# The two scans run alone with two copies of their staging tiles, and the local attention runs after them with the memory's keys and values between its blocks

## The chip, the cores and the metric

The kernel runs on one core of one Trainium2 chip. The core has a matrix engine (TensorE, PE in the profile), a vector engine (VectorE, DVE), a scalar engine (ScalarE, ACT), GpSimd (POOL) and SyncE (SP). SP issues all the transfers spoken of here, and 16 DMA engines carry them. The metric is the device time of one execution in microseconds.

## The reference, cut to what matters

One layer of an encoder over 2048 tokens of width 1024. One input projection feeds three groups of heads that don't depend on each other. Their results are joined by one output projection; a cross attention to 256 memory tokens and a feed-forward layer follow.

```python
h = rmsnorm(x, norm_mix_w[l])
(na_q, ..., ml_q, ..., gd_q, ...) = jnp.split(h @ w_in[l], IN_OFFSETS, axis=-1)
y_na = neighbourhood_attention(na_q, na_k, na_v, na_rel_bias[l])   # 6 heads of 64, window of 8 x 16 on a 32 x 64 grid
y_ml = mlstm_mixer(ml_q, ml_k, ml_v, ...)                          # 4 heads, one scan in each direction
y_gd = gated_deltanet_mixer(gd_q, gd_k, gd_v, ...)                 # 6 heads, one scan in each direction
x = x + jnp.concatenate([y_na, y_ml, y_gd], axis=-1) @ w_out[l]
x = x + memory_cross_attention(rmsnorm(x, norm_xa_w[l]), rmsnorm(mem, norm_mem_w[l]), w_xq[l], w_xkv[l], w_xo[l])
h = rmsnorm(x, norm_ffn_w[l])
x = x + jnp.square(jax.nn.relu(h @ w_ff1[l])) @ w_ff2[l]
```

## The kernel before

There are three passes. `pass_a` (to about 980 us) makes the input projection and what the scans need, and writes it to HBM: `kb_d`, `g_st`, `gd_c`, `w_d`, `sc_d`, `v_d` for the gated DeltaNet, `mlc_d`, `mlv_d`, `mx_row`, `ai_row` for the mLSTM, `nac_d`, `nav_d` for the local attention, `gate_d` for the output gates.

`pass_b` (about 985 to 1930 us) interleaves four generators:

- `gdn_scan`: 16 steps. Step m treats tile m (128 tokens) in the forward direction and tile 15-m in the backward one, each on its own half of the partitions. `load(m+1)` is written ahead of the step's arithmetic. It loads `wp`, `sc` and `qe` with one or two DMAs for each direction, and `kb` and `ge` with one DMA for both (line 666, in `both`). The source of `ge` is two rows of 768 numbers, one a direction, each read for 64 partitions; the source of `kb` is two blocks of 64 x 768. ScalarE takes the exponential of `ge` (line 647), GpSimd multiplies it into `sc` (line 650), TensorE makes products of `kb` and `wp` (line 658). The step has two halves, one for each chunk of 64 tokens, in a chain of three products and their copies (lines 681 to 702); each half waits for the state of the half before.
- `ml_scan`: the same shape for the mLSTM, with `mkq`, `mr_`, `mqe` and, as one DMA for both directions from two rows of 512 numbers, `mge` (line 851) and `me` (line 850). VectorE and GpSimd work on `me` (lines 852, 853). It runs one step behind (`LAG`).
- `na`: the local attention, 16 blocks of 128 queries. A block holds 6 heads, treated in three pairs; of a head the scores (line 977), bias and minimum (982), exponential (983), transposes (987), copies (990, 992) and the product with the values (997); at its end the sums' reciprocals (1000, 1004) and a store to `y_d` (1009). Bias tiles (947), values (953) and queries (956) are loaded a block ahead; the keys lie in a tile of 24 of the grid's 32 rows that is loaded anew at block 8.
- `heads_out`: for each of 16 tiles, once both directions have reached it, the norm of the heads, the gate `gz` (loaded in line 716) and a store to `y_d`. The first of the tiles can start at step 9.

A scheduler builds one instruction list for each engine from this program; tiles come from pools with a number of buffers (`bufs`), and a load into a tile waits until the last reader of the buffer is done. SP takes its list in order, so a DMA that waits for its buffer holds all the later ones.

After that `tail`: the memory is normed (`mem_in`), its keys and values are computed with `w_xkv` in 16 steps (`mem_kv`: 24 matmuls of 128 x 256 each, line 95), and the cross attention goes through four blocks of 512 tokens (`y_in` reads `y_d`, `mixed` applies `w_out`, then norm, queries, attention, output). In the first block four of the 16 key and value steps stand ahead of `w_out`, ten between the norm and the queries, and two behind them. From there to the end the kernel is matmuls with few gaps.

## Time and profile before

| what | value |
|---|---|
| median of 3 runs | 4131.57 us (4126.9 to 4132.66) |
| the profiled execution | 4129.29 us |
| its span | 4127.3 us |
| mean granted TensorE clock | 0.897 |
| TensorE busy | 3515.8 us (85%) |
| VectorE, ScalarE, GpSimd busy | 43%, 27%, 35% |
| DMA read and written | 331.16 MB, 92.12 MB |

The page cuts the span into 40 slices of 103 us and gives the busy share of each engine in tenths; the row of the granted clock and that of the DMA read alike. The scans are slices 10 to 19:

```
PE   5988999895357566663999999999999999999998
PEclk8989999995576766775999999999999999999999
DMA  4476425855343454533333333321111132111112
```

The chain that ended last is followed back from the last instruction: at each step to what released it. A share of that chain under a DMA's name is time in which the end of the kernel waited for this transfer.

### The profile page before, as it was taken

The numbers are of one execution on the slowest core, as the hardware profiler recorded it, in microseconds if no ns is written. First come the engines' busy times: TensorE is split into PE (matmuls) and PEld (weight loads), VectorE is DVE, ScalarE is ACT, GpSimd is POOL, SyncE is SP. The second block draws the span as 40 slices with busy tenths as digits, with TensorE's granted clock in tenths as the row PEclk, the third lists the DMA queues.
The fourth block names the chain that finished last, engine by engine and source line by source line (L and its number), as shares of the span: only waits on it lengthen the run. The fifth ranks groups of instructions, "written<-read, shape, count | busy, mean of one in ns | idle before, by whom it ended". The sixth has DMA issues, their size and how long they took to land.

```text
span 4127.3 us, 53735 instructions
## 1 busy us (share of the span) xinstructions
PE 3515.8 (85%) x21360; PEld 2830.8 (69%) x21360; DVE 1770.1 (43%) x3241; ACT 1122.2 (27%) x1976; POOL 1435.5 (35%) x876
## 2 busy tenths in 40 slices
PE   5988999895357566663999999999999999999998
PEld 4766777673235454442888888778888877888887
DVE  7767483741243345555443434532222244222224
ACT  3222422231122222221343333322221232221123
POOL 4242523441121112223544544433333354333333
PEclk8989999995576766775999999999999999999999
DMA  4476425855343454533333333321111132111112
GB/s 134 114 197 135 152 83 160 228 117 140 94 113 91 114 144 118 137 110 129 112 97 127 98 120 131 106 78 46 45 49 51 55 104 83 44 46 47 51 51 87
DMA packets 376610, 426.79 MB, mean 103 GB/s; under 512 B 150872, under 2 KB 277544, under 8 KB 374696
## 3 DMA queue, kind: packets, MB, share of 16 engines
q1 hardware_dynamic: 375816, 421.79, 34.8%
q8 instruction: 168, 2.75, 0.3%
q0 software_dynamic: 544, 1.57, 0.2%
q14 instruction: 82, 0.67, 0.1%
HBM read 331.16 MB, written 92.12 MB: 103 GB/s over the span
## 4 chain that ended last, share of the span: by engine, by line
PE 56%; DMA 13%; DVE 4%; SPq 3%; issue 2%; POOL 2%; ACT 1%; DVEq 0%; POOLq 0%; ACTq 0%
PE psg L95 31%; PE psa L95 19%; DMA ge<-g_st 4%; DMA me<-mx_row 3%; DMA wp<-w_d 1%; DMA y_d<-gz 1%; PE psn L977 1%; SPq L953 1%; PE psy L997 1%; PE psn L987 1%; DMA sc<-sc_d 1%; SPq L846 1%; DMA nav<-nav_d 0%; PE pss L688 0%; POOL wlo L1021 0%
## 5 line engine op out<-in xcount | busy, mean ns | idle before, releaser
L1021 POOL TENSOR_TENSOR wlo<-wraw,whi 128x1024 fp32r<-128x1024 f32 (+2 forms) x386 | 773.1, 2004 | 1367.0 <-ACT whi L1019 1328.7
L95 PE MATMUL psg<-acta,whi 128*128 128x512 f32 (+1 forms) x3008 | 951.9, 397 | 6.4 <-ACT acta L1160 3.2
L95 PE MATMUL psg<-actb,whi 128*128 128x512 f32 (+1 forms) x2752 | 841.6, 388 | 49.0 <-ACT actb L273 14.0
L1019 ACT CAST whi<-wraw 128x1024 fp32r<-128x1024 f32 (+2 forms) x402 | 358.1, 891 | 1230.6 <-PE psa L95 556.8
L95 PEld LDWEIGHTS psg<-acta,whi 128*128 128x128 f32 (+1 forms) x3008 | 567.8, 190 | 129.6 <-ACT acta L1160 4.0
L95 PE MATMUL psa<-ht,whi 128*128 128x512 f32 x2048 | 638.7, 395 | 0.7 <-ACT whi L1019 0.7
L95 PEld LDWEIGHTS psg<-actb,whi 128*128 128x128 f32 x2752 | 515.1, 192 | 158.1 <-ACT actb L273 14.7
L95 PE MATMUL psg<-acta,wlo 128*128 128x512 f32 (+1 forms) x1504 | 595.8, 397 | 1.8 <-POOL wlo L1021 1.8
L95 PE MATMUL psg<-actb,wlo 128*128 128x512 f32 (+1 forms) x1376 | 533.0, 387 | 4.7 <-POOL wlo L1021 4.2
L95 PEld LDWEIGHTS psa<-ht,whi 128*128 128x128 f32 x2048 | 384.1, 188 | 95.1 <-ACT whi L1019 1.6
L95 PE MATMUL psa<-ht,wlo 128*128 128x512 f32 x1024 | 400.8, 396 | 0.5 <-POOL wlo L1021 0.5
L1252 DVE TENSOR_TENSOR fr<-fr 128x512 f32<-128x512 f32 x128 | 167.8, 1311 | 495.6 <-ACT fr L1251 495.6
L1265 DVE TENSOR_TENSOR xb<-psa,xb 128x512 f32<-128x512 f32 x256 | 175.6, 691 | 475.9 <-PE psa L95 475.9
L95 PEld LDWEIGHTS psg<-acta,wlo 128*128 128x128 f32 (+1 forms) x1504 | 286.1, 190 | 64.4 <-POOL wlo L1021 3.3
L95 PEld LDWEIGHTS psg<-actb,wlo 128*128 128x128 f32 x1376 | 263.2, 191 | 57.4 <-POOL wlo L1021 5.8
L1255 POOL TENSOR_TENSOR ht<-fr,ht 128x512 fp32r<-128x512 f32 x128 | 168.9, 1320 | 250.2 <-ACT ht L1254 248.9
L95 PEld LDWEIGHTS psa<-ht,wlo 128*128 128x128 f32 x1024 | 192.2, 188 | 47.4 <-POOL wlo L1021 1.7
L853 POOL TENSOR_TENSOR me<-me,gm 128x512 f32<-128x512 f32 x16 | 21.1, 1320 | 456.9 <-DVE me L852 414.4
L987 PE MATMUL psn<-ident,nas 128*96 128x128 f32 (+1 forms) x336 | 75.6, 360 | 111.6 <-ACT nas L983 111.4
L308 DVE SCALAR_TENSOR_TENSOR acc<-pad,vecs,acc 128x512 f32<-128x512 f32 (+2 forms) x144 | 143.8, 1012 | 2.8
L1048 DVE TENSOR_TENSOR ss<-ss,sqt 128x512 f32<-128x512 f32 (+1 forms) x91 | 120.4, 1324 | 45.1 <-ACT sqt L1047 42.2
L997 PE MATMUL psy<-nap,nav 96*64 96x128 f32 (+2 forms) x672 | 89.3, 349 | 52.1 <-ACT nap L990 47.8
(376 smaller groups left out, 4042.3 us busy)
## 6 DMA issues: line engine op xcount, KB each, us to landing
wraw<-in_w_ff SPq DMA_DIRECT2D x72, 512.0 KB
wraw<-in_w_ff SPq DMA_DIRECT2D x144, 256.0 KB
wraw<-in_w_out SPq DMA_DIRECT2D x32, 512.0 KB
wraw<-in_w_xq SPq DMA_DIRECT2D x32, 512.0 KB
wraw<-in_w_xo SPq DMA_DIRECT2D x32, 512.0 KB
wraw<-in_w_gd SPq DMA_DIRECT2D x24, 512.0 KB
sc_d<-sc SPq DMA_DIRECT2D x32, 384.0 KB
sc<-sc_d SPq DMA_DIRECT2D x32, 384.0 KB
```

The costliest lines, as they stand in the source:

```text
L95: nc.tensor.matmul(out=out, lhsT=a(k), rhs=b(k), start=(i == 0), stop=(i == n - 1))
L308: V.scalar_tensor_tensor(out=acc[:, :n], in0=pad[:, p0 + j:p0 + j + n], scalar=cw(j), in1=acc[:, :n], op0=ALU.mult, op1=ALU.add)
L846: nc.sync.dma_start(out=kq[:, d], in_=self.mlc_d[t])
L953: nc.sync.dma_start(out=vw[:rows * ncl, j], in_=src)
L987: nc.tensor.transpose(out=tp[:n, P * j:P * j + P], in_=s[:, kt * j:kt * j + n], identity=self.ident)
L997: nc.tensor.matmul(out=yp[64 * e:64 * e + 64, P * hp:P * hp + P], lhsT=vw[:n, j, 128 * hp + 64 * e:128 * hp + 64 * e + 64], rhs=pts[e][:n, ...
L1019: nc.scalar.copy(out=hi, in_=raw)
L1021: (lo_eng or nc.gpsimd).tensor_tensor(out=lo, in0=raw, in1=hi.bitcast(F32), op=ALU.subtract)
L1048: nc.vector.tensor_tensor(out=ss, in0=ss, in1=sq, op=ALU.add)
L1252: V.tensor_tensor(out=r, in0=r, in1=r, op=ALU.mult)
L1255: G.tensor_tensor(out=ht[:, 1], in0=r, in1=ht[:, 0].bitcast(F32), op=ALU.subtract)
L1265: V.tensor_tensor(out=xs[nb][:, j], in0=ps, in1=xs[nb][:, j], op=ALU.add)
```

## The change

- `pass_b` holds the two scans and `heads_out` only. The pools of PSUM that the local attention had there are gone, `pss` has 4 buffers for 3 and `psl` 3 for 2.
- The staging tiles `kb`, `ge`, `qe`, `mqe`, `mge`, `mkq`, `me` and `gz` have two buffers for one.
- `na` runs in a new `pass_c` at the start of `tail`. It loads all keys with three DMAs (`nak`, 2048 columns a head pair), has four bias tiles for three, its transposes use a PSUM pool of their own (`pst`, 2 buffers) beside that of the scores (`psn`, 2), and the two heads of a pair are written one after the other.
- `mem_in` and `mem_kv` become `self.fill`, of which `pass_c` takes one step with every block of the local attention. The normed memory has its own tile.
- The tiles for the activations and for `x` are allocated after `pass_c`. The first block of the cross attention has nothing to fill the gap at its norm.

Seven lines fewer stand ahead of the scans, so line 647 becomes 640, 666 becomes 659 and so on; line 977 becomes 960 and line 95 becomes 94.

```diff
@@ -220,26 +219,20 @@
 
         with ExitStack() as st:
             pool = lambda name, bufs, **k: st.enter_context(self.pool(name, bufs, **k))
-            self.sps = pool("pss", 3, space=PSUM)
-            self.lps = pool("psl", 2, space=PSUM)
-            self.yps = pool("psy", 1, space=PSUM)
-            self.nps = pool("psn", 2, space=PSUM)
-            attn = self.na(pool("na", 2, side="right"))
+            self.sps = pool("pss", 4, space=PSUM)
+            self.lps = pool("psl", 3, space=PSUM)
             self.acc = pool("acc", 1).tile([P, 16, 10, 64], F32, name="acc")
             scan = self.gdn_scan(pool("scan", 2))
-            next(scan)
+            ml = self.ml_scan(pool("mls", 2))
             out = self.heads_out(pool("out", 2, side="right"))
-            next(out)
-            ml = self.ml_scan(pool("mls", 2))
+            for g in (scan, ml, out):
+                next(g)
             for m in range(16 + LAG):
                 next(scan, None)
                 if m >= LAG:
                     next(ml)
-                self.step(attn, 3)
                 if m - LAG >= 8:
                     self.step(out, 2)
-            for _ in chain(attn, out):
-                pass
 
     def norm_in(self, b):
 
...
@@ -632,9 +625,9 @@
-            kb = pool.tile([P, 2, 6, 64], F32, name="kb", bufs=1)
-            ge = pool.tile([P, 2, 6, 64], F32, name="ge", bufs=1)
-            qe = pool.tile([P, 6, P], F32, name="qe", bufs=1)
+            kb = pool.tile([P, 2, 6, 64], F32, name="kb")
+            ge = pool.tile([P, 2, 6, 64], F32, name="ge")
+            qe = pool.tile([P, 6, P], F32, name="qe")
...
@@ -711,7 +704,7 @@
-            gate = pool.tile([P, 5, P], F32, name="gz", bufs=1)
+            gate = pool.tile([P, 5, P], F32, name="gz")
...
@@ -837,10 +830,10 @@
-            qe = pool.tile([P, 4, P], F32, name="mqe", bufs=1)
-            ge = pool.tile([P, 4, P], F32, name="mge", bufs=1)
-            kq = pool.tile([P, 2, 4, P], F32, name="mkq", bufs=1)
-            e = pool.tile([P, 2, 4, 64], F32, name="me", bufs=1)
+            qe = pool.tile([P, 4, P], F32, name="mqe")
+            ge = pool.tile([P, 4, P], F32, name="mge")
+            kq = pool.tile([P, 2, 4, P], F32, name="mkq")
+            e = pool.tile([P, 2, 4, 64], F32, name="me")
...
@@ -876,6 +869,7 @@
         cur = load(0)
+        yield
...
@@ -921,18 +915,9 @@
-        def keys(parts):
-
-            ks = pool.tile([P, 3, 24 * 64], F32, name="nak", bufs=1)
-            at = 0
-            row = {}
-            for a, b in parts:
-                row.update({r: at + r - a for r in range(a, b)})
-                nc.sync.dma_start(out=ks[:, :, 64 * at:64 * (at + b - a)], in_=self.nac_d[3:6, :, 64 * a:64 * b].rearrange("j p l -> p j l"))
-                at += b - a
-            return ks, row
-
-        ks, row = keys(((4, 28),))
+        ks = pool.tile([P, 3, T], F32, name="nak", bufs=1)
+        for j in range(3):
+            nc.sync.dma_start(out=ks[:, j], in_=self.nac_d[3 + j])
...
@@ -943,7 +928,7 @@
-                    bt = pool.tile([P, 2, 480], F32, name="nab", bufs=3)
+                    bt = pool.tile([P, 2, 480], F32, name="nab", bufs=4)
...
@@ -963,25 +948,22 @@
-            if i == 8:
-                ks, row = keys(((0, 12), (20, 32)))
-            k0 = row[r0]
-                pts, sps = [], [self.nps.tile([P, 512], F32, name="psn") for _ in range(2)]
-                for sp, hb in zip(sps, (slice(0, 64), slice(64, 128))):
-                    nc.tensor.matmul(out=sp[:, :nk], lhsT=q[hb, hp], rhs=grid(ks)[hb, hp, k0:k0 + nr, c0:c0 + ncl], start=True, stop=True)
-                for sp, h in zip(sps, (2 * hp, 2 * hp + 1)):
+                pts = []
+                for h in (2 * hp, 2 * hp + 1):
+                    hb = slice(64 * (h % 2), 64 * (h % 2) + 64)
+                    sp = self.nps.tile([P, 512], F32, name="psn")
+                    nc.tensor.matmul(out=sp[:, :nk], lhsT=q[hb, hp], rhs=grid(ks)[hb, hp, r0:r0 + nr, c0:c0 + ncl], start=True, stop=True)
-                    tp = self.nps.tile([P, 512], F32, name="psn")
+                    tp = self.ntp.tile([P, 512], F32, name="pst")
...
@@ -1065,10 +1047,31 @@
             self.gemm_pools(ctx)
             self.sp = pool("nrm", 2)
             self.yp = pool("yr", 3)
+            self.kv = ExitStack()
+            kv = self.kv.enter_context(self.pool("kv", 1, side="right"))
+            self.kT = kv.tile([P, 2, KT, 256], F32R, name="kT")
+            self.vt = kv.tile([P, 2, 2, 1024], F32R, name="vt")
+            with self.pool("mem", 1) as p:
+                self.fill = chain(self.mem_in(p), self.mem_kv(p))
+                self.pass_c()
+                for _ in self.fill:
+                    pass
+            self.ap = pool("act", 1)
             self.xps = [pool("xa", 1), pool("xb", 1)]
             self.aps = pool("psa", 5, space=PSUM)
             self.cross()
             self.ffn(out)
+    def pass_c(self):
+        with ExitStack() as st:
+            pool = lambda name, bufs, **k: st.enter_context(self.pool(name, bufs, **k))
+            self.yps = pool("psy", 1, space=PSUM)
+            self.nps = pool("psn", 2, space=PSUM)
+            self.ntp = pool("pst", 2, space=PSUM)
+            for i, _ in enumerate(self.na(pool("na", 2, side="right"))):
+                if i % 3 == 1:
+                    self.step(self.fill, 1)
     def xtile(self, i):
         return self.xps[i].tile([P, KT, 512], F32, name="xb")
...
@@ -1089,32 +1092,23 @@
     def cross(self):
         with ExitStack() as ctx:
             self.x2_d = self.dr.tile([4, P, KT, 512], F32, name="x2_d")
-            kv = ctx.enter_context(self.pool("kv", 1))
             self.kp = ctx.enter_context(self.pool("xap", 2))
-            self.kT = kv.tile([P, 2, KT, 256], F32R, name="kT")
-            self.vt = kv.tile([P, 2, 2, 1024], F32R, name="vt")
-            with self.pool("mem", 1) as p:
-                self.mem_in(p)
             prev = None
             for i, b in enumerate(ORDER):
-                with self.pool("mkv", 3) as p:
-                    if i == 0:
-                        fill = self.mem_kv(p)
-                        self.step(fill, KV_FIRST)
-                    xb, ss = self.mixed(b, i)
-                    ha = self.act(0)
-                    self.norm_apply(xb, self.rms_bcast(ss, self.sp), 8, ha, self.sp)
-                    if i > 0:
-                        fill = self.xo(*prev)
-                    self.step(fill, 14 - KV_FIRST if i == 0 else 7)
-                    q = self.queries(ha, 0)
-                    for _ in fill:
-                        pass
+                xb, ss = self.mixed(b, i)
+                ha = self.act(0)
+                self.norm_apply(xb, self.rms_bcast(ss, self.sp), 8, ha, self.sp)
+                fill = self.xo(*prev) if prev else iter(())
+                self.step(fill, 7)
+                q = self.queries(ha, 0)
+                for _ in fill:
+                    pass
                 oa = self.act(1)
                 self.attend(ha, oa, q)
                 prev = b, oa, xb
             for _ in self.xo(*prev):
                 pass
+        self.kv.close()
 
     def mem_in(self, pool):
 
...
@@ -1123,7 +1117,8 @@
-        self.mem = self.act(1)
+        self.mem = pool.tile([P, 2, KT, 256], F32R, name="mem")
+        yield
...
@@ -1138,7 +1133,7 @@
-                tp = self.aps_tile()
+                tp = self.mps.tile([P, 512], F32, name="psm")
```

**SP in the scans.** The five tiles of one load of the DeltaNet scan have neighbouring numbers (`wp_10073`, `sc_10074`, `kb_10075`, `ge_10076`, `qe_10077`). SP before, from `kb` to the local attention's values and its store:

```order
L666 DMA kb_10075<-kb_d_80 128x1x768
L666 DMA ge_10076<-g_st_81 128x1x768
L849 DMA mqe_10215<-mlc_d_74 64x2x128 x4
L851 DMA mge_10216<-ai_row_5956 128x1x512
L956 DMA naqb_9948<-nac_d_76 128x3x128
L641 DMA wp_10073<-w_d01_85 64x768
L641 DMA wp_10073<-w_d12_90 64x768
L846 DMA mkq_10217<-mlc_d_74 128x512 x2
L850 DMA me_10218<-mx_row_5955 128x1x512
L953 DMA nav_9943<-nav_d_77 128x1x384
L1009 DMA y_d1_69<-nat_9685 128x3x128
L953 DMA nav_9943<-nav_d_77 128x1x384 x2
```

SP after, at the same place of a step:

```order
L659 DMA kb_9650<-kb_d_80 128x1x768
L659 DMA ge_9651<-g_st_81 128x1x768
L840 DMA mr__9789<-mlv_d_75 64x2x260 x2
L842 DMA mqe_10300<-mlc_d_74 64x2x128 x4
L844 DMA mge_10301<-ai_row_5956 128x1x512
L634 DMA wp_9393<-w_d01_85 64x768
L634 DMA wp_9393<-w_d12_90 64x768
L839 DMA mkq_10302<-mlc_d_74 128x512 x2
L843 DMA me_10303<-mx_row_5955 128x1x512
```

The local attention's `naqb`, `nav` and `y_d1` are gone from between the scans' loads. Before, `kb` and `ge` of a load stand ahead of the `wp` of that load; after, `kb_9650` and `ge_9651` stand ahead of `wp_9393`, the tile of the load before.

**VectorE at the first norm of the cross attention.** Line 1082 (1085 after) adds a product of `w_out` to `xb`, line 78 (77) begins the norm's factor, line 1037 (1019) applies it; `kT` and `wlo` belong to the memory's keys. VectorE before:

```order
L1082 TENSOR_TENSOR xb<-psg,xb 128x512
L1021 TENSOR_TENSOR wlo<-wraw,whi 128x1024
L1048 TENSOR_TENSOR ss<-ss,sqt 128x512
L1137 TENSOR_TENSOR kT<-psg,kT 128x256
L78 TENSOR_SCALAR ms<-psm 128x4
L1021 TENSOR_TENSOR wlo<-wraw,whi 128x1024
L1137 TENSOR_TENSOR kT<-psg,kT 128x256
L1037 SCALAR_TENSOR_TENSOR nh<-xb,vecs,psm 128x512 x3
L1137 TENSOR_TENSOR kT<-psg,kT 128x256
L1039 TENSOR_TENSOR acta<-nh,acta 128x512
L1037 SCALAR_TENSOR_TENSOR nh<-xb,vecs,psm 128x512 x2
```

VectorE after:

```order
L1085 TENSOR_TENSOR xb<-psg,xb 128x512
L1030 TENSOR_TENSOR ss<-ss,sqt 128x512
L1085 TENSOR_TENSOR xb<-psg,xb 128x512
L1030 TENSOR_TENSOR ss<-ss,sqt 128x512
L77 TENSOR_SCALAR ms<-psm 128x4
L1019 SCALAR_TENSOR_TENSOR nh<-xb,vecs,psm 128x512 x3
L1021 TENSOR_TENSOR acta<-nh,acta 128x512
L1019 SCALAR_TENSOR_TENSOR nh<-xb,vecs,psm 128x512 x3
L1021 TENSOR_TENSOR acta<-nh,acta 128x512
```

Before, work for the keys (`kT`, `wlo`) stands among the norm's instructions; after, only the norm's own do, and the queries (`xq`) come next.

**PE in the local attention.** `psn` are scores, `pst` transposes, `psy` the product with the values, `mem` is the normed memory. PE before, in the scans:

```order
L977 MATMUL psn<-nak,naqb 128x480 x2
L658 MATMUL pss<-wp,kb 64x64 x21
L898 MATMUL psl<-mr__9444,msc 64x65 x8
L658 MATMUL pss<-wp,kb 64x64 x3
L987 MATMUL psn<-ident,nas 128x128 x3
L987 MATMUL psn<-ident,nas 96x128
L681 MATMUL pss<-sc,wp 64x64 x12
L987 MATMUL psn<-ident,nas 128x128 x3
L987 MATMUL psn<-ident,nas 96x128
```

PE after, in its second block:

```order
L960 MATMUL psn<-nak,naqb 128x360
L94 MATMUL psg<-mem,whi 128x256 x3
L94 MATMUL psg<-mem,wlo 128x256
L94 MATMUL psg<-mem,whi 128x256 x2
L94 MATMUL psg<-mem,wlo 128x256
L94 MATMUL psg<-mem,whi 128x256
L979 MATMUL psy<-nap,nav 64x128 x6
L969 MATMUL pst<-ident,nas 96x128 x3
```

The rows of the scans (lines 658 and 681) that filled the places between scores and transposes are gone; rows of `mem` stand there instead, in the first eleven of the 16 blocks.

## Rows read from the trace of the kernel before

**Rows 1.** The page, part 4: the chain that ended last, shares by engine, then by line.
```profile
PE 56%; DMA 13%; DVE 4%; SPq 3%; issue 2%; POOL 2%; ACT 1%; DVEq 0%; POOLq 0%; ACTq 0%
PE psg L95 31%; PE psa L95 19%; DMA ge<-g_st 4%; DMA me<-mx_row 3%; DMA wp<-w_d 1%; DMA y_d<-gz 1%; PE psn L977 1%; SPq L953 1%; PE psy L997 1%; PE psn L987 1%; DMA sc<-sc_d 1%; SPq L846 1%; DMA nav<-nav_d 0%; PE pss L688 0%; POOL wlo L1021
```

**Rows 2.** Waits, 1000 to 1920 us: engine, its line, what released it: total us, times, longest.
```profile
ACT ge L647 <- DMA ge<-g_st: 272.4, 16, 28.3
DVE me L852 <- DMA me<-mx_row: 185.1, 15, 38.8
```

**Rows 3.** Chain of waits, 1280 to 1400 us: start us, length us, what.
```profile
1297.56 19.75 DMA ge<-g_st
...
1325.51 8.94 DMA me<-mx_row
...
1355.37 19.48 DMA ge<-g_st
```

**Rows 4.** Stretches: us, busy us of each engine (instructions), PEclk, DMA share, GB/s.
```profile
1050.00:1790.00 740.00, 452.52 (x5477) 334.93 (x5473) 316.76 (x755) 185.68 (x471) 147.99 (x96) 0.69 0.43 116
1311.00:1316.00 5.00, 0.00 (x0) 0.00 (x0) 0.00 (x0) 0.00 (x0) 0.00 (x0) 0.50 0.13 52
1786.00:1930.00 144.00, 59.80 (x604) 44.15 (x602) 84.42 (x243) 23.52 (x51) 33.97 (x22) 0.62 0.28 86
1968.00:2012.00 44.00, 43.79 (x197) 36.03 (x195) 19.94 (x14) 12.48 (x16) 20.55 (x9) 1.00 0.30 98
```

**Rows 5.** DMA issues, 1050 to 1790 us: out<-in, count, KB each.
```profile
kb<-kb_d SPq DMA_DIRECT2D x14, 384.0 KB
ge<-g_st SPq DMA_DIRECT2D x14, 384.0 KB
...
mge<-ai_row SPq DMA_DIRECT2D x13, 256.0 KB
...
me<-mx_row SPq DMA_DIRECT2D x12, 256.0 KB
...
nav<-nav_d SPq DMA_DIRECT2D x21, 192.0 KB
...
nav<-nav_d SPq DMA_DIRECT2D x22, 144.0 KB
...
naqb<-nac_d SPq DMA_DIRECT2D x13, 192.0 KB
y_d<-nat SPq DMA_DIRECT2D x13, 192.0 KB
```

**Rows 6.** Line 683, 985 to 1930 us: ns min/median/max, first and last start.
```profile
L683 DVE COPY sc<-pss x32: 518/549/551, 1052.2 to 1785.9; 64x384 f32<-64x384 f32 x32
```

**Rows 7.** TensorE by line, 985 to 1930 us, the local attention: count | busy, mean.
```profile
L977 PE MATMUL psn<-nak,naqb 64*128 64x480 f32 (+5 forms) x184 | 95.3, 642 | 0.4 <-ACT nay L1006 0.4
L997 PE MATMUL psy<-nap,nav 96*64 96x128 f32 (+2 forms) x656 | 86.6, 347 | 52.1 <-ACT nap L990 47.8 <-DVE nap L990 4.1
L987 PE MATMUL psn<-ident,nas 128*128 128x128 f32 (+1 forms) x324 | 72.6, 357 | 110.2 <-ACT nas L983 110.0
...
L1004 PE MATMUL psn<-ident,nsm 128*64 128x128 f32 x192 | 19.5, 332 | 10.2 <-DVE nsm L1000 10.2
```

**Rows 8.** Chain of waits, 1786 to 1930 us, the scans' tail.
```profile
1810.71 8.73 DMA me<-mx_row
...
1926.10 2.78 DMA y_d<-gz
```

**Rows 9.** TensorE in order of time, 1940 to 2066 us, memory keys: start us, us, count.
```profile
1963.24 0.40 PE L95 MATMUL psg<-actb,whi 128*128 128x256 f32 x2
...
1966.11 0.40 PE L95 MATMUL psg<-actb,whi 128*128 128x256 f32 x2
```

**Rows 10.** VectorE and ScalarE in order of time, 2008 to 2050 us, the first cross norm.
```profile
2014.93 0.68 DVE L1048 TENSOR_TENSOR ss<-ss,sqt 128x512 f32<-128x512 f32 x1
...
2024.05 1.94 ACT L1038 CAST acta<-nh 128x512 fp32r<-128x512 f32 x3 [0.43 <-DVE nh L1037]
```

More of the change, by code (lines that the diff above doesn't have):

```diff
@@ L35 @@
 ORDER = (1, 2, 0, 3)
-KV_FIRST = 4
 class Trunk:
@@ L138, in gemm_pools @@
         self.wp, self.wb = ctx.enter_context(self.pool("wst", 2, side="right")), 2
-        self.ap = ctx.enter_context(self.pool("act", 1, side="right"))
     def pass_a(self):
@@ L145, in pass_a @@
             self.gemm_pools(st)
+            self.ap = pool("act", 1, side="right")
             self.acts = [None, None]
@@ L1000, in na @@
             V.reciprocal(out=sm, in_=sm)
-            tp = self.nps.tile([P, 512], F32, name="psn")
+            tp = self.ntp.tile([P, 512], F32, name="pst")
             for hp in range(3):
```

## The prediction, made before the changed kernel ran

> **What bounds the kernel now.** I read the chain of waits first. Over half of it is TensorE and 13% are transfers, and the two largest of these belong to the scans, `ge` with 4% and `me` with 3% of the span [rows 1]: some 290 us in which the end of the kernel waited for two small tiles. The change works on the stretch that holds them, the scans, so I ask what sets the pace there. In 740 us of it TensorE is busy for 452 and VectorE for 317, at a granted clock of 0.69; the DMA engines for 0.43 [rows 4]. No engine is the bound by these shares. The waits name the transfers again: ScalarE's line 647 waits 272 us for `ge` in 16 steps and VectorE's line 852 waits 185 us for `me` [rows 2]; one `ge` takes 19 to 20 us at the end of the chain and one `me` 9 [rows 3].
>
> The question that decides the case is why 384 KB take 19 us. From 1311 to 1316 us every engine is idle, ScalarE waits for `ge` (its wait runs from 1297.56 to 1317.31, [rows 3]), and the DMA share is 0.13 with 52 GB/s [rows 4]. 0.13 of 16 engines is two engines. So `ge` is not late because it is issued late; it is slow because two engines carry it. `kb` is written in the same way (two blocks, one for each direction), and so are `me` and `mge`.
>
> A step of the scans takes 47.3 us: the evacuation of line 683 runs from 1052.2 (first half of step 0) to 1785.9 (second half of step 15), which is 15.5 steps [rows 6]. I set this against the two engines. Their own four transfers are 384 + 384 + 256 + 256 KB = 1.31 MB a step [rows 5], at 52 GB/s **25.2 us**. All transfers together keep 0.43 of the engines busy, which is 20.3 us of all 16 for each step; the four take 25.2 x 2/16 = 3.2 of that, and the other 17.1 us, spread over all 16, pass through these two engines too. Sum 42.3 of 47.3 us. The scans before are bound by two DMA engines, with 5 us of slack.
>
> **The change part by part.**
>
> *Doubled tiles.* A second buffer lets `kb`, `ge`, `me` and their like be issued a step earlier, so it hides a delay. It does not make the two engines carry less. It is worth the 5 us of slack at most, and part of it will stay, since `ge` of the next load still stands in one queue behind other tiles that wait for their buffers (in the SP rows `kb_9650` and `ge_9651` come one load ahead of `wp_9393`, and the `sc` of the load before comes after). I take 4 us gained, bounds 0 and 5. `gz` doubled takes its wait out of the tail, below.
>
> The Trainium skill, page "DMA: Bandwidth & Descriptors", section "Why a DMA increments its semaphore by 16 and not by 1", says that a transfer is spread over the largest number of engines up to 16 that divides the slowest dimension of both its sides, and that a transfer issued by an engine's own queue takes the lowest-numbered ones. A source whose outermost dimension is two then runs on two engines, and four such transfers on the same two; the idle stretch with its share of 0.13 agrees with the first half, and no row here shows which engines they are. If the four spread over different pairs, the sum would be that of the first rival.
>
> *The local attention leaves the scans.* Its values, queries and stores are 21 x 192 + 22 x 144 + 13 x 192 + 13 x 192 KB = 12.5 MB in these 740 us [rows 5], 0.8 MB a step of some 4.2 MB that are not the four; bias tiles and keys come on top. I take 5 us of the 17.1, bounds 3 and 7. Its arithmetic beside the scans was not on the path: no engine is full. So a step goes from 47.3 to 47.3 - 4 - 5 = **38 us**, bounds 35 (25.2 + 17.1 - 7, no slack) and 44. From step 9 the heads' `gz` loads and stores join, in fact now in each step: 5 us more, 43. The first two steps find their tiles loaded, and the last two have no loads behind them; for them I go by TensorE's own work, (452 - 275 x 0.8) / 15.7 = 15 us (13 of the 16 blocks lie there) [rows 4, 7], and by 43 on the other side, and take 29. From the first evacuation at 1052: 2 x 29 + 7 x 38 + 4 x 43 + 2 x 29 = 554, so step 15 begins at 1606 and its last half at 1616, against 1785.9. **Gain 170 us**, bounds 60 and 215.
>
> *The tail of the scans.* Before, 142 us pass from 1785.9 to 1928; VectorE is busy for 84 of 144 there, and the rest is waits such as 8.7 us for `me` and 2.8 for a store of `gz` [rows 4, 8]. After, four pairs of heads and three mLSTM steps are left. VectorE's part without the local attention's (some 10 us) for 8 tiles of heads where there were 10 is about 62, and 10 us of waits stay: 72, bounds 60 and 90. The scans end at **1688**, bounds 1630 and 1810, against 1928: 240 us earlier.
>
> *The local attention alone.* This is what it costs. TensorE spent 95 + 87 + 73 + 20 = 275 us on it, at a clock of 0.69 [rows 4, 7], hidden under the scans. At full clock that is 189 us if all of it went with the clock and 275 if none did; I take 205, since matmuls mostly go with it. The memory's keys and values as filler are 8 triples in 2.87 us [rows 9], 128 triples in all, 46 us. So TensorE alone needs 250 us, and it has nothing else to hide behind. The stage cannot be as tight as `w_out` (43.8 busy of 44, [rows 4]): a head is a chain over TensorE, VectorE and ScalarE, line 987 sat idle 110 us for the exponential and line 997 52 us before [rows 7], and the PE rows show that the filler ends with the eleventh of the 16 blocks. I take 300 us, bounds 265 and 360 (some clock lost), and 9 us for its first loads, since keys, bias and values are issued behind the last stores. It ends at 1688 + 9 + 300 = **1997**.
>
> *The join.* Before, the keys and values and 48 matmuls of the queries are done at 2064.9. After, from the end of the local attention: 2.5 us for its last store (a like one took 2.8, [rows 8]), 13 for reading `y_d` behind the loads of `x` (an estimate; in the rows before, the memory's keys hide it), 44 for `w_out` [rows 4], 9 to 12 for the norm, which runs from the last sum at 2014.9 to the first cast at 2024.1 [rows 10] and which nothing covers now, and 16 for the queries. Together 87.5, so the break-even is an end of the local attention at 1977. At 1997 the change **costs 20 us**. From there on the two kernels do the same.
>
> 4129.3 + 20 = 4149 for the profiled execution; the median of the runs before is 2.3 us above it, which makes 4152.
>
> **The rivals.** (a) *Faster.* The scans give more than I take: the two engines are served without a break (35 us a step) and the tail takes 60, so the scans end near 1650, and the local attention stays at full clock with 270 us. It then ends at 1650 + 9 + 270 = 1929, 48 us before the break-even: 4083. If the four slow transfers were on two different pairs of engines, a step's floor would be 25.2 / 2 + 12.1 = 25 us, 13 less in each of 11 steps, and the time about 4010. For it: TensorE is idle for 288 of 740 us in the scans [rows 4], so its own work would allow it. Against it: 42 of 47 us are accounted for by one pair of engines.
>
> (b) *No change.* The same gain in the scans and a stage of 280 us: the end lies at 1977, and the two cancel, 4131.
>
> (c) *Slower by more.* The local attention alone doesn't keep TensorE busy enough; the clock falls as in the scans (0.69) and its stage takes 360 us: 80 us past the break-even, 4212. It decides from the point at which the filler ends.
>
> (d) *The staging tiles don't do what they are for.* If SP's list holds `ge` behind a tile that is not free, so that only the loads' share (5 us) is gained, steps take 42 and 47, the scans end 11 x 4 = 44 us later than in the forecast, and the time is about 4196.
>
> **How the numbers follow.** My forecast, slower by some 10 to 60 us: 0.46. (a) 0.26, (b) 0.14, (c) 0.08, (d) 0.06. The likeliest time is 4152. Cases on both sides of no change hold the chance; the forecast's own range is 4140 to 4190. The range that should hold the time 8 times in 10 leaves out the far ends of (a) and of (c) and (d): 4070 to 4230. About 0.2%, 8 us, is what a measurement of this kernel can tell from no change. Faster by more than that 0.26, within it 0.14, slower 0.60.
>
> **What would show it.** Line 676 (683 before) should step by 37 to 40 us up to step 8 and by about 43 with the heads; its wait in ScalarE for `ge` should be shorter but there, and in idle stretches the DMA share should again be 0.13. The scans should end between 1650 and 1730. The local attention should take 280 to 330 us with a clock above 0.85 and its last five blocks should show TensorE waiting for the exponential. Before the first norm of the cross attention TensorE should stand idle for about 10 us. Wrong would be: steps of less than 33 us (then the two engines were not the bound), a local attention of less than 270, or a scan stage that is no shorter.

## The result, and the profile after

| | before | after |
|---|---|---|
| median | 4129.61 us (4126.9 to 4132.66) | 4187.28 us (4182.47 to 4192.22) |
| span of the profiled execution | 4127.3 us | 4186.8 us |
| mean granted clock | 0.897 | 0.903 |
| ratio, with its 95% interval | | 1.014 [1.0122, 1.0157] |

The change made the kernel slower by 57.7 us. The direction is the one forecast, but the loss that was forecast was 22 us (4152). The page after, with the rows that answer to [rows 1]: three of the rows of 40 slices (105 us each), then the chain that ended last.

```profile
PE   5988999893233335499799999999999999999998
...
PEclk8999999895566667599899999999999999999999
DMA  4476435844243344345323233321111132111112
...
PE 54%; DVE 2%; issue 1%; ACT 1%; DMA 1%; POOL 1%; SPq 0%; POOLq 0%; DVEq 0%; ACTq 0%
PE psg L94 30%; PE psa L94 19%; PE psn L960 2%; PE psy L979 1%; PE pst L969 1%; DVE ss L1030 0%; PE psm L75 0%; PE psa L1198 0%; DMA xb<-x_d 0%; PE psm L85 0%; PE pst L986 0%; ACT whi L1001 0%; DMA me<-mx_row 0%; DVE gz L727 0%; POOL wlo L1
```

Slices 11 to 17 are the scans with their tail, 18 and 19 the local attention, 20 the join: TensorE goes from 2 to 5 tenths to 9, and then to 7. The transfers have left the chain: 13% of it before, 1% after, and `ge` no longer stands among the entries that are shown. Read alone, that looks like a wait that was cured. It was not. The shares of the chain add up to 60% of the span, where they were 81%. In the stretch ahead of the local attention the chain's pieces begin only near 1654, in the last two steps of the scans, so it was not followed into the steps before:

```profile
1654.63 0.78 DVE acc L721
...
1752.03 8.44 issue
1760.47 1.59 PE psn L960 x4
```

The waits between 1000 and 1760 us (engine, line, what released it; total us, times, longest), against [rows 2]:

```profile
ACT ge L640 <- DMA ge<-g_st: 290.6, 16, 27.4
...
DVE me L845 <- DMA me<-mx_row: 227.8, 13, 49.1
```

ScalarE waits longer for `ge` than before, and VectorE for `me`, with two buffers each. The pace of the scans is read from line 676, which was 683 [rows 6]:

```profile
L676 DVE COPY sc<-pss x32: 539/546/552, 1074.1 to 1672.0; 64x384 f32<-64x384 f32 x32
```

(1672.0 - 1074.1) / 15.5 = 38.6 us a step, where it was 47.3. That is an average: the single steps run from 59.3 us (the first) to 24.5.

Six stretches (us, busy us of PE, PEld, DVE, ACT and POOL, granted clock, DMA share, GB/s): one inside the wait for `ge` that the line ahead of them shows (ScalarE idle for 27.27 us, up to 1194.04), the local attention, its first and its last part, and the two gaps behind it.

```profile
1194.04 0.84 ACT L640 ACTIVATE ge<-ge 128x768 f32<-128x768 f32 x1 [27.27 <-DMA ge<-g_st]
...
1179.00:1183.00 4.00, 0.00 (x0) 0.00 (x0) 0.00 (x0) 0.00 (x0) 0.00 (x0) 0.50 0.13 52
1760.00:2008.00 248.00, 245.34 (x1801) 165.32 (x1802) 105.24 (x322) 133.85 (x380) 28.76 (x18) 0.95 0.47 144
1760.00:1800.00 40.00, 38.94 (x189) 23.10 (x191) 20.38 (x58) 20.37 (x59) 7.35 (x8) 0.69 0.60 194
1930.00:2008.00 78.00, 76.40 (x584) 47.64 (x584) 32.83 (x118) 43.91 (x136) 4.85 (x3) 1.00 0.47 138
2008.00:2040.00 32.00, 17.45 (x58) 11.73 (x59) 4.83 (x5) 7.00 (x11) 11.86 (x8) 0.79 0.66 206
2071.00:2084.00 13.00, 6.12 (x22) 4.58 (x21) 5.76 (x7) 3.47 (x5) 5.17 (x4) 0.66 0.20 72
```

In the first every engine is idle, the DMA share is 0.13 and 52 GB/s move, as in [rows 4]: 0.13 of 16 is two, so two DMA engines carry `ge`, before and after. In the second TensorE is busy for 245 of 248 us, the first 40 of them at a clock of 0.69, and in the last part, which the memory's products reach for 9 us only (the last is at 1938.8), for 76.4 of 78. In the last two it is idle for 14.5 and 6.9 us. What it waits for there, from the chain of waits (start, length, what):

```profile
2007.36 0.57 DVE nat L990
...
2015.36 3.36 SPq L1150
...
2018.82 7.00 DMA yr<-y_d
...
2038.54 32.71 PE psg L94 x139
...
2072.96 2.38 DVE ss L1030
...
2080.71 0.76 DVE nh L1019
```

The local attention ends at 2007.4 to 2007.9; SP then issues the loads of `x` and a piece of `y_d` (line 1150) that lands at 2025.8; `w_out` runs to 2071; the norm takes from 2073.0 to the first normed piece at 2081.5.

The last loss lies where nothing was expected. TensorE's groups in 400 us of the feed-forward (count | busy us, mean ns of one), before and then after:

```profile
L95 PE MATMUL psa<-ht,whi 128*128 128x512 f32 x596 | 186.5, 395 | 0.7 <-ACT whi L1019 0.7
...
L95 PE MATMUL psg<-acta,whi 128*128 128x512 f32 x288 | 88.8, 389 | 0.0
L95 PE MATMUL psg<-actb,whi 128*128 128x512 f32 x256 | 78.8, 389 | 0.0
```

```profile
L94 PE MATMUL psa<-ht,whi 128*128 128x512 f32 x582 | 182.0, 395 | 0.6 <-ACT whi L1001 0.6
...
L94 PE MATMUL psg<-acta,whi 128*128 128x512 f32 x288 | 90.3, 394 | 0.0
L94 PE MATMUL psg<-actb,whi 128*128 128x512 f32 x256 | 80.0, 393 | 0.0
```

Before, a matmul of 512 columns takes 395 ns when it streams `ht` and 389 when it streams `acta` or `actb`. After, all three take 393 to 395. The granted clock is 1.00 in both.

Laid out on the time axis, with the forecast's own marks:

| mark | before | forecast | after |
|---|---|---|---|
| first evacuation of the scans | 1052 | 1052 | 1074 |
| last half step | 1786 | 1616 | 1672 |
| scans and heads done | 1928 | 1688 | 1751 |
| local attention, start to end | in the scans | 1697 to 1997 | 1760 to 2008 |
| first scores of the cross attention | 2070.6 | +20 | 2097.9 (+27.3) |
| end of the span | 4127.3 | +20 | 4186.8 (+59.5) |

### The profile page after: what moved, and what is told of

Its sections match the earlier page's. It is cut to its first block, busy times and chain, and to the rows that moved or that the text cites. A ratio compares the mean times of both kernels' runs of the same rounds, so it can differ in the third digit from the quotient of the medians.

```text
span 4186.8 us, 53799 instructions
## 1 busy us (share of the span) xinstructions
PE 3492.6 (83%) x21360; PEld 2802.8 (67%) x21360; DVE 1778.6 (42%) x3241; ACT 1120.4 (27%) x1976; POOL 1435.6 (34%) x876
## 4 chain that ended last, share of the span: by engine, by line
PE 54%; DVE 2%; issue 1%; ACT 1%; DMA 1%; POOL 1%; SPq 0%; POOLq 0%; DVEq 0%; ACTq 0%
PE psg L94 30%; PE psa L94 19%; PE psn L960 2%; PE psy L979 1%; PE pst L969 1%; DVE ss L1030 0%; PE psm L75 0%; PE psa L1198 0%; DMA xb<-x_d 0%; PE psm L85 0%; PE pst L986 0%; ACT whi L1001 0%; DMA me<-mx_row 0%; DVE gz L727 0%; POOL wlo L1003 0%
## 5 line engine op out<-in xcount | busy, mean ns | idle before, releaser
L94 PE MATMUL psg<-acta,whi 128*128 128x512 f32 (+1 forms) x3008 | 967.0, 402 | 22.4 <-ACT acta L1155 16.2
L94 PE MATMUL psg<-actb,whi 128*128 128x512 f32 x2496 | 796.5, 399 | 40.7 <-ACT actb L266 13.8
L94 PEld LDWEIGHTS psg<-actb,whi 128*128 128x128 f32 x2496 | 470.5, 190 | 156.3 <-ACT actb L266 14.6
L94 PE MATMUL psg<-actb,wlo 128*128 128x512 f32 x1248 | 499.5, 401 | 2.9 <-POOL wlo L1003 2.9
L94 PEld LDWEIGHTS psg<-actb,wlo 128*128 128x128 f32 x1248 | 236.5, 190 | 59.7 <-POOL wlo L1003 4.1
L674 PE MATMUL pss<-sc,wp 128*64 128x64 f32 x768 | 48.1, 278 | 210.8 <-ACT sc L684 190.2
L674 PEld LDWEIGHTS pss<-sc,wp 128*64 128x64 f32 x768 | 40.7, 185 | 217.4 <-ACT sc L684 194.1
L681 PE MATMUL pss<-sc 128*64 128x64 f32 x744 | 53.8, 291 | 116.3 <-DVE sc L676 98.0
L1030 DVE TENSOR_TENSOR ss<-ss,sqt 128x512 f32<-128x512 f32 (+1 forms) x91 | 122.4, 1345 | 49.1 <-ACT sqt L1029 45.9
```

The lines of the kernel that those rows point to most:

```text
L94: nc.tensor.matmul(out=out, lhsT=a(k), rhs=b(k), start=(i == 0), stop=(i == n - 1))
L674: nc.tensor.matmul(out=ps[CH[d], 64 * h:64 * h + 64], lhsT=wp[:, d, cc[d], h], rhs=sc[:, d, cc[d], 2, h], start=True, stop=True)
L681: nc.tensor.matmul(out=ps[SR[d], 64 * h:64 * h + 64], lhsT=sc[:, d, cc[d], 1, h], rhs=sc[:, d, cc[d], 2, h], start=True, stop=True)
L1030: nc.vector.tensor_tensor(out=ss, in0=ss, in1=sq, op=ALU.add)
```

## The experiments

### What sets the pace of the scans

Two kernels change how the disputed transfers are written and nothing else: each of `kb`, `ge`, `me` and `mge` is loaded by one DMA for each direction, so that its outermost dimension is 64 and not 2. The same bytes move, in twice as many DMAs.

```diff
-            nc.sync.dma_start(out=out, in_=in_)
+            for i, rows in enumerate(CH):
+                nc.sync.dma_start(out=out[rows], in_=in_[i])
...
-            nc.sync.dma_start(out=e.rearrange("p c h l -> p (c h l)"), in_=self.mx_row.rearrange("d t c h l -> (d t) (c h l)")[m:32 - m:31 - 2 * m, None].broadcast_to([2, 64, 512]))
+            for i, rows in enumerate(CH):
+                nc.sync.dma_start(out=e[rows].rearrange("p c h l -> p (c h l)"), in_=self.mx_row.rearrange("d t c h l -> (d t) (c h l)")[m:32 - m:31 - 2 * m, None].broadcast_to([2, 64, 512])[i])
```

**b_split**, in the kernel before, with its single buffers:

> The kernel before with one edit: kb, ge, me and mge are each loaded by two DMAs, one for each direction, with 64 partitions as the outermost dimension, so that all 16 DMA engines carry them. Nothing else changes, the staging tiles stay single. Theory (two DMA engines set the pace of the scans): the 25.2 us a step that these four transfers take on two engines become some 6 us on sixteen, the share of the DMA engines in waits for ge is no longer 0.13, a step falls from 45.7 to about 33 us, the scans end 130 to 200 us earlier, time 3940 to 4010. Rival (the loads are late because their buffers come free late, which doubling cures): the time of one ge falls but the step stays above 42 us, time 4100 to 4130.

Measured: 3873.21 us against 4131.32, ratio 0.9384 [0.936, 0.9409]. The rival (4100 to 4130) is out by 227 us. The evacuation of the first product, the two waits and the stretch of the scans, in this kernel's lines:

```profile
L684 DVE COPY sc<-pss x32: 537/549/550, 1019.7 to 1541.2; 64x384 f32<-64x384 f32 x32
```

```profile
DVE me L854 <- DMA me<-mx_row: 59.9, 13, 14.6
ACT ge L647 <- DMA ge<-g_st: 58.0, 11, 11.4
...
1040.00:1541.00 501.00, 396.66 (x5297) 295.32 (x5296) 313.48 (x740) 179.05 (x456) 144.73 (x93) 0.79 0.66 164
```

33.6 us a step (521.5 / 15.5) where it was 47.3, and 58 us of waits for `ge` where there were 272 [rows 2]. The DMA engines are busy for 0.66 of the scans and move 164 GB/s, where it was 0.43 and 116 [rows 4]. The edit changes the number of DMAs along with their outermost dimension; the two were not tried apart.

**a_split**, in the changed kernel:

> The changed kernel with the same edit (kb, ge, me and mge by one DMA a direction). Theory (two engines are the floor that doubled tiles left): a step falls from 37.8 to 22 to 28 us, which the engines' own chain then sets, the scans end 130 to 200 us earlier, time 3990 to 4060. Rival (the step after the change is already bound by the engines' chain): step 35 us or more, time 4140 to 4190.

Measured: 3907.82 us, ratio to before 0.946 [0.9446, 0.9474], 279 us less than the changed kernel.

```profile
L677 DVE COPY sc<-pss x32: 533/546/550, 1005.2 to 1393.0; 64x384 f32<-64x384 f32 x32
```

```profile
ACT ge L640 <- DMA ge<-g_st: 83.0, 11, 12.4
...
DVE me L847 <- DMA me<-mx_row: 70.2, 13, 11.9
```

25.0 us a step where it was 38.6 (the expectations count from the second half of step 0, which gives 24.7 and 37.8). Both times lie below the range expected, by 67 and 82 us. The steps give 13.7 x 15.5 = 212 and 13.6 x 15.5 = 211 us. Most of the rest is the start, which I had left out: the first evacuation comes 32 and 69 us earlier (1019.7 for 1052.2, 1005.2 for 1074.1). That makes 244 of the 258 us in the one and all of the 279 in the other.

**What the doubled tiles are worth.** a_one takes them back in the changed kernel:

```diff
-            kb = pool.tile([P, 2, 6, 64], F32, name="kb")
+            kb = pool.tile([P, 2, 6, 64], F32, name="kb", bufs=1)
```

and so for `ge`, `qe`, `mqe`, `mge`, `mkq`, `me` and `gz`.

> The changed kernel with the eight staging tiles (kb, ge, qe, mqe, mge, mkq, me, gz) back at one buffer; the local attention stays behind the scans. Theory (two DMA engines set the pace, doubling takes only the slack): a step goes from 37.8 to 40 to 43 us, time 4187 plus 40 to 90, 4225 to 4280. Rival (doubling is what shortened the step, the attention's departure did nothing): a step of 46 us, time 4310 or more.

Measured: 4221.31 us, ratio to before 1.0219 [1.0201, 1.0238], 34 us more than the changed kernel, just below the range. The step, and the start of the local attention with what TensorE waited for ahead of its scores:

```profile
L676 DVE COPY sc<-pss x32: 537/548/551, 1046.0 to 1674.1; 64x384 f32<-64x384 f32 x32
```

```profile
L960 PE MATMUL psn<-nak,naqb x192: 382/560/967, 1788.8 to 2022.9; 64*128 64x360 f32 x48, 64*128 64x480 f32 x48, 64*128 64x264 f32 x24, 64*128 64x352 f32 x24
...
  DVE gz L727: 24.0, 1
```

A step is 40.5 us (628.1 / 15.5): of the 8.7 us that the change took off a step, 6.8 came with the local attention's leaving (the two PSUM buffers that the scans got by it were not tried alone) and 1.9 from the doubled tiles. The last half step is at 1674 without them and at 1672 with them, since the first comes 28 us earlier without (1046.0 for 1074.1). What is lost lies behind the scans: the scores of the local attention start at 1788.8 for 1760.5, behind 24.0 us of waiting for the last work on `gz`, and end 20 us later, of the 22 by which this profiled execution is longer. So what the doubling was worth lies with `gz`, the tile of the heads, by this wait; `gz` alone was not put back.

a_split_one does the same in a_split.

> As a_split (kb, ge, me and mge by one DMA a direction, so on sixteen DMA engines; 24.7 us a step, 3908), with the eight staging tiles at one buffer. Theory: once the transfers are short, the delay between a free buffer and a landed tile is what is left, and doubling hides it: a step of 28 to 34 us, time 3960 to 4040. Rival (with sixteen engines the loads are hidden without doubling): 24 to 26 us a step, 3900 to 3920.

Measured: 3945.69 us, between the two ranges. The theory fell on its reason and not only on its size:

```profile
L677 DVE COPY sc<-pss x32: 535/548/551, 1004.3 to 1388.8; 64x384 f32<-64x384 f32 x32
```

24.8 us a step, the same as with two buffers. With the transfers split the loads are hidden without doubling, as the rival said; the last half step comes at 1389 for 1393, so the 38 us that single buffers cost lie behind the scans again.

### Why the same matmuls took longer

In the built programs `acta` and `actb` of the last pass start at 172000 and 139232 (bytes in a partition) before and at 38208 and 70976 after; the weights `whi` at 212960 in both. `ht`, the hidden tiles of the feed-forward, is the third operand of this kind. Seven kernels move some of these tiles by unused bytes ahead of a pool, as a_pad2720 does (a_wpad has them ahead of the weights' pool):

```diff
+            pool("pad", 1).tile([P, 680], F32, name="pad")
             self.ap = pool("act", 1)
```

> The changed kernel with 32 unused bytes a partition allocated ahead of the activations' tiles in the last pass, so that acta and actb start at 38240 and 71008 instead of 38208 and 70976 (ht, kT's neighbours and x move by 32 bytes too). Theory (where the moving operand starts in SBUF, in steps of 32 bytes, costs TensorE 3% of a matmul of 512 columns): the matmuls on acta and actb go from 0.2335 to 0.227 us each, those on ht too, time 4187 less 25 for acta and actb less up to 19 for ht, 4140 to 4165. Rival (the side of the memory on which the tiles lie, or what else runs at the time, costs it): no change, 4182 to 4192.

> The kernel before with 32 unused bytes a partition ahead of x's tiles in the last pass: acta and actb stay where they are, ht starts at 87392 instead of 87360 and so on. Theory (start address modulo 64): the 3072 matmuls on ht go from 0.2333 to 0.227 us, time 4130 less 19, about 4111. Rival (ht is slower for another reason, as its tile's size or its output): no change.

> The changed kernel with 2720 unused bytes a partition ahead of the activations' tiles, so that acta and actb start at 40928 and 73696, which leaves the same remainder after division by 8192 (8160) as their place in the kernel before (172000, 139232); ht starts at 155616 and has the remainder 2016 after division by 2048, as acta had. Theory (the remainder of the moving operand's start decides a 3% cost of TensorE's matmuls): those on acta and actb at 0.227 us again, those on ht too if 2048 is the measure, time 4187 less 25, or less 25 and 19: 4135 to 4170. Rival (the place itself, far from the weights or near, decides): no change, 4178 to 4192.

> As b_split (3873), with 672 unused bytes a partition ahead of x's tiles in the last pass, so that ht starts at 88032, remainder 2016 after division by 2048, as acta and actb; these stay where they are. Theory (remainder after division by 2048): the matmuls on ht at 0.227 us, time 3873 less 19, 3850 to 3860. Rival (another measure): ht at 0.233 us, 3868 to 3880.

> As a_split_pad2720 (3855), with 704 unused bytes: acta and actb start at 38912 and 71680, ht at 153600 and so on, all multiples of 2048, so that a row of 512 numbers crosses no multiple of 2048. Theory (a crossing inside the row costs TensorE 7 ns, and one 32 bytes from its start is hidden): as a_split_pad2720, matmuls 0.227 us or less apart, 3850 to 3860. Rival (the remainder has to equal that of the weights' tiles, 2016): 0.233 us apart, 3895 to 3910.

> As a_split_pad2720, with 1728 unused bytes: acta and actb start at 39936 and 72704, remainder 320 after division by 1024 is gone, the remainder after division by 2048 is 1024 and a row crosses a multiple of 2048 at its middle. Theory (a crossing inside the row): 0.233 us between matmuls, 3895 to 3910. Rival (a multiple of 1024 is enough): 0.227 us, 3850 to 3860.

> The changed kernel with 672 unused bytes ahead of the weights' tiles: the activations of the last pass stay where the change put them (acta 38208, actb 70976, ht 152896: remainder 1344 after division by 2048), the weights (whi, wlo) move from 212960 to 212288, remainder 1344 too; the first pass's activations move along with the weights. Theory (weights and moving operand must have the same remainder after division by 2048): 0.227 us between matmuls on acta, actb and ht, as in a_pad2720, 4130 to 4145. Rival (the remainder 2016 of the moving operand itself): 0.233 us everywhere, the first pass too, 4195 to 4215.

The remainders are those of the tile's start after division by 2048. The distance is the mean from one start to the next of consecutive matmuls of 512 columns in the feed-forward, from the trace.

| kernel | weights | `acta`, `actb` | `ht` | distance `acta`, `ht` (ns) | time (us) |
|---|---|---|---|---|---|
| before | 2016 | 2016 | 1344 | 227.1, 233.4 | 4129.6 |
| b_pad32 | 2016 | 2016 | 1376 | 226.8, 233.3 | 4129.1 |
| b_split_pad672 | 2016 | 2016 | 2016 | 226.7, 226.7 | 3855.4 (b_split: 3873.2) |
| after | 2016 | 1344 | 1344 | 233.3, 233.3 | 4187.3 |
| a_pad32 | 2016 | 1376 | 1376 | 233.5, 233.3 | 4179.5 |
| a_pad2720 | 2016 | 2016 | 2016 | 226.7, 226.7 | 4136.7 |
| a_split_pad704 | 2016 | 0 | 0 | 233.3, 233.3 | 3900.8 (a_split: 3907.8) |
| a_split_pad1728 | 2016 | 1024 | 1024 | 233.4, 233.3 | 3902.1 |
| a_wpad | 1344 | 1344 | 1344 | 226.7, 226.7 | 4137.7 |

The theory of 32 bytes fell with the first two (a_pad32 is 8 us faster than the changed kernel, with the two spreads overlapping and the distances unchanged), and that of a row that crosses a multiple of 2048 with a_split_pad704, where no row crosses one and the distances stay at 233.3 ns (its time is 7 us lower, which the distances don't explain). a_wpad settles that the place of one operand relative to the other decides: the activations stay where the change put them, the weights move to the same remainder, and all is fast.

How fine the measure is, the table does not say, and 2048 is not shown to be it. A matmul reads one slice of 128 columns (512 bytes) of the weights' tile and one of 512 columns (2048 bytes) of the activations'. From one of the eight slices to the next the weights' remainder thus moves on by 512 and the other stays. Yet before the change all eight run alike, with mean distances of 226.6 to 227.0 ns for `acta`. So for the single matmul equal remainders after division by 512 are enough. Division by 512 or by 256 fits every row of the table; division by 128 does not, since 1376 and 2016 both leave 96 and a_pad32 is slow. Between 512 and 256 no run decides.

The groups of a_pad2720 and then of a_wpad, 400 us of the feed-forward in each:

```profile
L94 PE MATMUL psa<-ht,whi 128*128 128x512 f32 x632 | 193.7, 390 | 0.9 <-ACT whi L1001 0.9
...
L94 PE MATMUL psg<-acta,whi 128*128 128x512 f32 x261 | 80.4, 389 | 0.0
```

```profile
L94 PE MATMUL psa<-ht,whi 128*128 128x512 f32 x634 | 194.3, 390 | 1.0 <-ACT whi L1002 1.0
...
L94 PE MATMUL psg<-acta,whi 128*128 128x512 f32 x258 | 79.4, 389 | 0.0
```

and of a_split_pad704, where the remainders differ:

```profile
L94 PE MATMUL psa<-ht,whi 128*128 128x512 f32 x536 | 167.9, 396 | 0.7 <-ACT whi L1003 0.7
...
L94 PE MATMUL psg<-acta,whi 128*128 128x512 f32 x320 | 101.8, 399 | 0.0
```

The price: 3072 + 2304 matmuls on `acta` and `actb` behind the local attention x 6.2 ns = 33 us, which the change pays and the kernel before doesn't. The 3072 on `ht` pay 20 us in both by the same working; b_split_pad672 got back 18. a_pad2720 gets both back: 54 by this sum, 50.6 measured. Why the place matters was not found.

### Both mends, and the gap at the join

> The changed kernel with both mends: kb, ge, me and mge by one DMA a direction (a_split, 3908) and 2720 unused bytes ahead of the activations' tiles (a_pad2720, 51 us less than the changed kernel). If the two are independent, 3908 less 45 to 50: 3855 to 3865, the same as the kernel before with both mends (b_split_pad672, 3855): the serial order is then worth nothing either way. Rival (in the shorter kernel part of the one gain is hidden by the other): 3875 or more.

Measured: 3855.5 us, ratio to before 0.9339 [0.9319, 0.936]. The serial order is then worth nothing either way: the kernel before with the same two mends has 3855.44.

a_best gives `yr`, the tile for the pieces of `y_d`, eight buffers for three, so that SP holds the loads of `y_d` ahead of those of `x`; its unused bytes are 672 in place of 2720, since the new buffers move the activations too:

```diff
-            self.yp = pool("yr", 3)
+            self.yp = pool("yr", 8)
```

> As a_split_pad2720, with 672 unused bytes in place of 2720 and eight buffers for yr in place of three, so that the eight loads of y_d for the first block stand ahead of the local attention's last stores on SP and of the loads of x. Theory (after the change TensorE stands idle between the local attention and w_out for 14.5 of 32 us, since the loads of y_d wait behind x on SP's queue): 10 to 15 us less than a_split_pad2720, 3840 to 3850, TensorE idle for under 4 us there. Rival (what it waits for is the last store of the local attention itself): 0 to 3 us less.

Measured: 3844.32 us, ratio to before 0.9313 [0.9293, 0.9333]. The 32 us from the end of the local attention:

```profile
1724.00:1756.00 32.00, 29.71 (x125) 22.61 (x124) 10.37 (x11) 11.11 (x18) 18.41 (x10) 1.00 0.80 268
```

TensorE is idle for 2.3 of 32 us, where it was 14.5 of 32 after the change. This is the fastest of the kernels here: 285 us less than the kernel before, 343 less than the changed one.

## Why the prediction was right or wrong

**Two DMA engines set the pace of the scans: right, and shown.** Splitting the four transfers freed 13 us a step in either kernel. On average the steps took what the sum said: steps 2 to 12 lasted 435 us together, for a forecast of 438. Step by step they did not, and that the sums agree is in part luck: steps 2 to 8 took 42.6 us each (38 forecast, 37 to 40 given as the sign) and steps 9 to 12 took 34.2 (43 forecast). Single steps of 30.8 and 24.5 us lie below the 33 that were named as a sign against the two engines, and the forecast had no term for so uneven a pace; what makes it was not found. The runs agree with the first half of what is cited from the Trainium skill (page "DMA: Bandwidth & Descriptors", section "Why a DMA increments its semaphore by 16 and not by 1"): a source of outermost dimension two moved at 52 GB/s with a share of 0.13, and with 64 the scans moved 164 GB/s. Which two engines carry a transfer was not read here; that all four queue on the same pair is not shown, though steps near 38 us fit it and the 25 us of different pairs do not.

**The ends of the scans: wrong by 56 us.** The term "the first two steps find their tiles loaded" failed: I took 58 us, and they took 59.3 + 32.3 = 91.6, and the first evacuation came 22 us late, at 1074, where I had kept it at 1052. What held the first evacuation stands in three rows of the trace:

```profile
1045.26 1.55 PE L674 MATMUL pss<-sc,wp 128*64 128x64 f32 x24
...
1073.38 0.69 DVE L845 TENSOR_TENSOR me<-cmx,me 128x512 f32<-128x512 f32 x1 [49.11 <-DMA me<-mx_row]
1074.10 0.55 DVE L676 COPY sc<-pss 64x384 f32<-64x384 f32 x1
```

The product was ready at 1046.8, before the 1052 of the forecast. But in VectorE's list the mLSTM's `me` now stands right ahead of the evacuation, and VectorE waited 49.1 us for that tile, one of the four slow transfers; the product lay for 27 us. With doubled tiles three of the mLSTM's loads of `me` are issued ahead of the first `wp`, where it was one, so the same transfers were only paid for earlier; this last step is argued (in a_one, with single buffers, the first evacuation is at 1046). Steps 2 to 8 took 298 us for 266, steps 9 to 12 137 for 172: the 5 us a step for the heads were not seen.

**The tail of the scans:** 79 us for 72. Right in kind and size.

**The local attention alone: too dear by 52 us.** The stage took 248 us, below the 270 that were named as a sign of being wrong. I had 250 us of TensorE work and put 50 on top for waits and clock, and 9 ahead. The 250 were right to 5 us (245), the 50 were not there: TensorE was busy 99% at a clock of 0.95. The last five blocks, which were to show it waiting for the exponential, did not: in the last 78 us, nearly without the memory's keys, it was busy 98%. So the filler is not what covers the waits for the exponential. That the second PSUM pool does, since scores and transposes of different heads can be under way together, is argued and was not tried; I had costed the stage from the waits [rows 7] of a kernel without it.

These errors nearly cancel, 56 + 7 late and 52 early: 2008 for 1997. That is luck.

**The join: right.** From the end of the local attention to the first scores of the cross attention it is 89.9 us; the forecast's mark lay 5.7 us ahead of these scores (2064.9 for 2070.6), so 84 us stand against 87.5. The gap at the norm is there. a_best shows that 12 of the 21 us of idle TensorE there came from the order of SP's queue.

**"From there on the two kernels do the same": wrong, and this is the step that failed.** The forecast put the rest of the kernel at nothing, and it cost 32 us: 27.3 us were lost at the first scores of the cross attention, 59.5 at the end. The change moved the activations' tiles to another place in SBUF, which stands in the diff as a pool that changes sides, and I costed that line at nothing. With the place mended (a_pad2720 and a_wpad, less the 18 us that `ht` gains in them) the change costs about 25 us. That is close to the forecast of 22, but only since the errors ahead of the join cancel.

**The rivals.** (a) wanted 35 us a step and 270 us for the local attention. The stage came in below that, the steps did not (38.6); steps of 25 us, its second form, came only when the transfers were split. (b) took the scans' end at 1688, and it was 1751. (c), a low clock in the local attention, did not happen beyond its first 40 us. (d) is close to what the tiles did, 1.9 us a step, though not for the reason named there.

## What to carry to other kernels

Before a slow transfer gets a second buffer, read the DMA share while nothing else runs. Here a share of 0.13 said that two of 16 engines carry it. Writing the DMA so that its outermost dimension is 64 gave 258 us, where second buffers gave 1.9 us a step and lost them again at the start. A chain of waits that loses an entry is not a proof that the wait is gone: after the change the total wait for `ge` had grown. Where a change moves a pool to another place, compare the start of the streamed tiles with that of the weights; a line without work in it cost 3% of 5400 matmuls. And where two chains share an engine, look at what its list puts ahead of the first link: a finished product lay 27 us behind another chain's wait.

## What the runs showed of the hardware that I had not expected

- A matmul of 512 fp32 columns came every 226.7 to 227.1 ns where the tiles of its moving operand and of its weights start at the same remainder after division by 2048 bytes (2016 or 1344 both), and every 233.3 to 233.5 ns for the four other pairs tried (1344, 1376, 0 and 1024 against 2016). Moving either one cures it (a_pad2720, a_wpad). The slices within the tiles show that division by 512 would do.
- The local attention's small matmuls kept TensorE at a granted clock of 1.00 from 1800 us on, its last 78 us nearly without the memory's products, though the first 40 us of the stage were at 0.69.
